# Attention scores of two transformer blocks: from plain fp32 matmuls head by head to three fp32r passes over high and low parts

## The chip, the cores and the metric

One core of a Trainium2 chip runs the whole kernel. The metric is device microseconds of one execution. Engines are called as in the profile: PE is TensorE's matmuls, PEld its weight loads, DVE is VectorE, ACT is ScalarE, POOL is GpSimd, SP issues most DMAs.

## What is computed

One sequence of 256 tokens, width 1024, passes through two blocks, all in fp32. The first block mixes with two attentions of 8 heads of 64 and gates them, then runs a layer that picks experts by product keys (PEER). The second block mixes with a causal attention and a gated spatial unit, then runs a gated feed-forward of 2816. The scores are three einsums:

```python
# first block, sliding window: 8 query heads on 2 key heads
logits = jnp.einsum('bcqhgd,bckhd->bhgcqk', qc, kw) * (HEAD_DIM ** -0.5)
logits = logits - slopes[None, :, :, None, None, None] * dist
probs = jax.nn.softmax(jnp.concatenate([logits, sink], axis=-1), axis=-1)[..., :-1]
# first block, stick-breaking: 8 heads
z = jnp.einsum('bqhd,bkhd->bhqk', q_blk, k) * (dh ** -0.5)
log_beta = jax.nn.log_sigmoid(z)
log_keep = jnp.where(before, jax.nn.log_sigmoid(-z), 0.0)
suffix = lax.cumsum(log_keep, axis=3, reverse=True) - log_keep
weights = jnp.where(before, jnp.exp(log_beta + suffix), 0.0)
# second block: with 256 tokens and blocks of 256, plain causal attention of 8 heads
s = jnp.einsum('bhqd,bhqnkd->bhqnk', qc, kg) * scale
p = jax.nn.softmax(jnp.where(mask, s, NEG_INF_2), axis=-1)
```

## The kernel before

The tokens are two blocks of 128 (NB = 2). Weights stream in units of 512 KB: `load` (line 80) issues the DMA on SP, ACT copies the unit into a high part in fp32r (line 91) and DVE takes the rest as a low part (line 92). Every projection is three fp32r matmuls, high by high, high by low, low by high (`mm3`, lines 97 to 100), feature-major (`fm`, 256 columns a matmul) or token-major (`tm`, 512 columns). `split` (line 123) makes the same two parts of an activation.

The scores alone are plain fp32. Queries and keys stand transposed, features on partitions, and two heads share the 128 partitions: head group g = 0 has partitions 0 to 63, g = 1 has 64 to 127. `swa(b, g)` (line 284), `sticks(b, g)` (line 318) and `attend(b, g)` (line 792) each take a query block b and four heads. For each head they issue one fp32 matmul of 64 rows and then a 16-bit matmul of 128 rows that adds the mask (for the sliding window the slope times distance, lines 293, 327 and 800). Block b reads n = 128 (b + 1) keys. The scores of four heads fill one double bank of the accumulator memory, tag "lg", of which there are two; the banks "mm" (two) serve the projections and "ms" (two) the transposes.

After the scores come the softmax (DVE maximum, ACT exponentials) or, in `sticks`, two sigmoids on ACT and a scan and a product on DVE. A `tail` then transposes the weights (`weighted`, line 266), multiplies them with the values into the same double bank, and splits the result into yaH, yaL or ybH, ybL.

The order in the first block: `qkb(i)` makes queries (i < 2) and keys (i >= 2, times the token's scale `rrow`) of the stick-breaking heads; `head_norm` and `head_turn` those of the sliding window. Two swa calls stand between the qkb units; then the values (pv), then a loop of eight steps, each with a tail, the scores of a later group, and a `gate_pair(i)`: two feature-major units whose products leave the bank by a DVE multiplication (line 363) and a sigmoid. In the second block the projections 0 (queries), 1 (keys), 4 (z), 3 (u) and 2 (values) run in this order; `rope` turns queries and keys; the scores of block 0 stand behind projection 4, those of block 1 behind projection 3.

The order on each engine is fixed at build time: a scheduler takes, of the instructions that it holds ready, the one that comes first in the program, so matmuls of a gate pair fill the gaps that attention leaves. `tc.issue_after` and `tc.high_priority` bend that order.

Of the kernel before, what the change touches and what calls it, by code (L numbers as in the profile page):

```python
# [9 lines left out]
F32 = mybir.dt.float32  # L10
# [8 lines left out]
P = 128  # L19
# [27 lines left out]
def block_kernel(ctx, tc, a, out):  # L47
# [101 lines left out]
    # ================= mixer of the first block =================  # L149
    with tc.tile_pool(name="b1", bufs=1) as b1:  # L150
# [30 lines left out]
        def x_part(i):  # L181
            # two chunks of the features of all tokens, times their gains
# [41 lines left out]
        qkn = b1.tile([P, NB, 10, HD], F32, name="qkn")  # L224
        va = b1.tile([P, NB, 2 * HD], F32, name="va")
        qaT = b1.tile([P, 4, S], F32, tag="qaT", name="qaT")
        kaT = b1.tile([P, S], F32, name="kaT")
        qkbT = b1.tile([P, 8, S], F32, tag="qkbT", name="qkbT")
        vb = b1.tile([P, NB, 512], F32, tag="vb", name="vb")
# [3 lines left out]
        ybH = b1.tile([P, 4, S], F32R, name="ybH")  # L233
        ybL = b1.tile([P, 4, S], F32R, name="ybL")
# [19 lines left out]
        def head_turn(b):  # L254
# [29 lines left out]
        def swa(b, g):  # L284
            # heads 4g .. 4g + 3 read key head g
            n = P * (b + 1)
            t = slice(b * P, b * P + P)
            r = slice(64 * g, 64 * g + 64)
            tile_ = pair()
            lg = quarters(tile_)  # L290
            for i in range(4):
                pe.matmul(lg[:, i, 0:n], qaT[r, i, t], kaT[r, 0:n], start=True, stop=False)  # L292
                pe.matmul(lg[:, i, 0:n], slopes[:, 4 * g + i, :], dist[:, b, 0:n], start=False,
                          stop=True)
            sm = b1.tile([P, 6, 4], F32, tag="sm", bufs=3, name="sm")
            sk = sinks[:, 4 * g:4 * g + 4]
            dve.tensor_reduce(sm[:, 0, :], lg[:, :, 0:n], axis=AX.X, op=ALU.max)
            dve.tensor_tensor(sm[:, 0, :], sm[:, 0, :], sk, op=ALU.max)
            dve.tensor_scalar_mul(sm[:, 1, :], sm[:, 0, :], -1.0)
            dve.tensor_sub(sm[:, 2, :], sk, sm[:, 0, :])  # L300
            pr = t4([P, 4, S], name="pr")
            act.activation(sm[:, 3, :], sm[:, 2, :], AF.Exp)
            for i in range(4):
                act.activation(pr[:, i, 0:n], lg[:, i, 0:n], AF.Exp, bias=sm[:, 1, i:i + 1],
                               accum_out=sm[:, 4, i:i + 1])
            dve.tensor_tensor(sm[:, 4, :], sm[:, 4, :], sm[:, 3, :], op=ALU.add)
            dve.reciprocal(sm[:, 5, :], sm[:, 4, :])

            def tail():
                y = tile_[:, 0, 0:256]  # L310
                weighted(pr, b + 1, lambda sb, i: va[:, sb, g * HD:g * HD + HD], y)
                ys = b1.tile([P, 4, HD], F32, tag="ys", bufs=2, name="ys")
                dve.tensor_tensor(ys, y.rearrange("p (h d) -> p h d", d=HD),
                                  sm[:, 5, :, None].to_broadcast([P, 4, HD]), op=ALU.mult)
# [3 lines left out]
        def sticks(b, g):  # L318
            # heads g, g + 2, g + 4, g + 6
            n = P * (b + 1)  # L320
            t = slice(b * P, b * P + P)
            r = slice(64 * g, 64 * g + 64)
            tile_ = pair()
            lg = quarters(tile_)
            for i in range(4):
                pe.matmul(lg[:, i, 0:n], qkbT[r, i, t], qkbT[r, 4 + i, 0:n], start=True, stop=False)  # L326
                pe.matmul(lg[:, i, n - P:n], identb, strict, start=False, stop=True)
            keep, beta, suf = t4([P, 4, S]), t4([P, 4, S]), t4([P, 4, S])
            pool.memset(suf[:, :, n - 1:n], 1.0)
            act.activation(keep[:, :, 0:n], lg[:, :, 0:n], AF.Sigmoid,  # L330
                           scale=rms8[:, b, 1:2])
            act.activation(beta[:, :, 0:n], lg[:, :, 0:n], AF.Sigmoid,
                           scale=rms8[:, b, 0:1])
            for i in range(4):
                dve.tensor_tensor_scan(suf[:, i, 0:n - 1][:, ::-1], keep[:, i, 1:n][:, ::-1],
                                       zero[:, 0:n - 1], 1.0, op0=ALU.mult, op1=ALU.add)
# [810 lines left out]
```

## Time and profile before

| | |
|---|---|
| timed runs | 1322.13, 1322.47, 1324.13 us; median 1322.47 us |
| profiled execution, span from the first to the last instruction | 1319.7 us |
| its own time | not listed beside the span; the median of the timed runs lies 2.8 us above the span |
| PE / PEld / DVE / ACT / POOL busy | 1295.5 / 1168.7 / 847.7 / 712.4 / 36.7 us |
| mean granted clock of TensorE | 0.994 of full speed |

Busy time adds up an engine's instructions, overlaps left out. A matmul's row shows its whole passage through the array; matmuls overlap one another, so the price of one in a stream is the distance from its start to the next start. "PEclk" is the granted clock, 1.00 for 2.4 GHz. What ended an engine's idle time is written behind the row as [idle <- releaser].

### The profile page before, as it was taken

How to read it: one execution, taken by the hardware profiler on the slowest of the kernel's cores; microseconds unless marked ns; L12 is line 12 of the kernel's file. 1: busy time of each engine (PE TensorE's matmuls, PEld its weight loads, DVE VectorE, ACT ScalarE, POOL GpSimd, SP SyncE). 2: the span in 40 equal slices, each digit the busy share in tenths (PEclk: the TensorE clock that was granted, in tenths of full speed). 3: DMA queues.
4: the chain of work that ended last, by engine and by line, in shares of the span. 5: the costliest groups of instructions: out<-in, count | busy, mean ns of one | idle time of the engine just before them, and what ended most of it. 6: DMA issues, size and time to landing. Idle time of an engine off the chain costs nothing.

```text
span 1319.7 us, 21851 instructions
## 1 busy us (share of the span) xinstructions
PE 1295.5 (98%) x8612; PEld 1168.7 (89%) x8612; DVE 847.7 (64%) x1440; ACT 712.4 (54%) x1166; POOL 36.7 (3%) x44
## 2 busy tenths in 40 slices
PE   8999999999999999999999999999999999999997
PEld 7888978999999999999988888888887778899996
DVE  5555685499987777777655555555555757545555
ACT  6474454444558777777544444544453464444443
POOL 2200000000000000000000000000000121000000
PEclk9999999999999999999999999999999999999999
DMA  8532464544555444454565665565666544455552
GB/s 297 176 96 96 138 214 149 190 153 159 184 161 179 157 161 160 160 161 160 178 195 196 195 194 192 191 193 194 193 197 202 192 147 151 150 179 189 189 181 94
DMA packets 65478, 229.11 MB, mean 174 GB/s; under 512 B 8288, under 2 KB 9056, under 8 KB 65248
## 3 DMA queue, kind: packets, MB, share of 16 engines
q1 hardware_dynamic: 64800, 226.54, 52.5%
q8 instruction: 67, 1.10, 0.3%
q10 hardware_dynamic: 576, 1.18, 0.3%
q14 instruction: 35, 0.29, 0.1%
HBM read 226.64 MB, written 1.05 MB: 173 GB/s over the span
## 4 chain that ended last, share of the span: by engine, by line
PE 89%; DVE 6%; ACT 2%; DMA 2%; issue 1%; POOL 0%; POOLq 0%; DVEq 0%; ACTq 0%
PE ps_mm L98 15%; PE ps_mm L100 15%; PE ps_mm L99 15%; PE ps_lg L99 12%; PE ps_lg L98 12%; PE ps_lg L100 12%; DVE wl L92 2%; PE ps_lg L655 1%; PE ps_lg L657 1%; PE ps_ms L132 1%; PE ps_lg L281 1%; DMA raw<-in_w_dram 1%; PE ps_lg L799 1%; PE ps_lg L292 1%; PE ps_lg L326 1%
## 5 line engine op out<-in xcount | busy, mean ns | idle before, releaser
L92 DVE TENSOR_TENSOR wl<-raw,wh 128x1024 fp32r<-128x1024 f32 (+1 forms) x385 | 470.9, 1226 | 328.5 <-ACT wh L91 327.7
L91 ACT ACTIVATE wh<-raw 128x1024 fp32r<-128x1024 f32 (+1 forms) x385 | 405.0, 1053 | 431.1 <-PE ps_lg L99 212.2
L98 PE MATMUL ps_mm<-xh,wh 128*128 128x256 f32 x1408 | 401.8, 285 | 0.0
L100 PE MATMUL ps_mm<-xh,wl 128*128 128x256 f32 x1408 | 398.6, 283 | 2.0 <-DVE wl L92 1.9
L99 PE MATMUL ps_mm<-xl,wh 128*128 128x256 f32 x1408 | 398.3, 283 | 0.0
L100 PEld LDWEIGHTS ps_mm<-xh,wl 128*128 128x128 f32 x1408 | 269.8, 192 | 2.6 <-DVE wl L92 2.6
L99 PEld LDWEIGHTS ps_mm<-xl,wh 128*128 128x128 f32 x1408 | 270.0, 192 | 0.7
L98 PEld LDWEIGHTS ps_mm<-xh,wh 128*128 128x128 f32 x1408 | 269.8, 192 | 0.7
L98 PE MATMUL ps_lg<-wh,sp 128*128 128x512 f32 x496 | 193.0, 389 | 0.0
L99 PE MATMUL ps_lg<-wl,sp 128*128 128x512 f32 x496 | 193.0, 389 | 0.0
L100 PE MATMUL ps_lg<-wh,sp 128*128 128x512 f32 x496 | 192.9, 389 | 0.0
L100 PEld LDWEIGHTS ps_lg<-wh,sp 128*128 128x128 f32 x496 | 93.1, 188 | 19.4
L99 PEld LDWEIGHTS ps_lg<-wl,sp 128*128 128x128 f32 x496 | 93.1, 188 | 19.3
L98 PEld LDWEIGHTS ps_lg<-wh,sp 128*128 128x128 f32 x496 | 93.1, 188 | 19.1
L641 ACT ACTIVATE oh<-oh,gL 128x128 f16<-128x128 f16 x256 | 83.6, 429 | 2.2 <-DVE oh L639 1.9
L98 PE MATMUL ps_mm<-hh,wh 128*128 128x256 f32 x192 | 56.1, 292 | 1.8 <-DVE gates L363 1.8
L100 PE MATMUL ps_mm<-hh,wl 128*128 128x256 f32 x192 | 55.0, 286 | 0.5 <-DVE wl L92 0.5
L99 PE MATMUL ps_mm<-hl,wh 128*128 128x256 f32 x192 | 54.7, 285 | 0.0
L125 DVE TENSOR_TENSOR sp<-store,sp 128x512 fp32r<-128x512 f32 x62 | 42.4, 684 | 0.2 <-ACT sp L124 0.2
L98 PEld LDWEIGHTS ps_mm<-hh,wh 128*128 128x128 f32 x192 | 36.6, 191 | 3.0 <-DVE gates L363 2.4
L124 ACT ACTIVATE sp<-store 128x512 fp32r<-128x512 f32 x62 | 38.0, 613 | 0.4 <-DVE store L668 0.4
L626 ACT ACTIVATE store<-ps_mm 128x512 f32<-128x512 f32 (+31 forms) x60 | 27.1, 451 | 19.6 <-DVE store L624 15.0
(369 smaller groups left out, 1701.8 us busy)
## 6 DMA issues: line engine op xcount, KB each, us to landing
raw<-in_u_dram SPq DMA_DIRECT2D x128, 512.0 KB, 3.5
raw<-in_v_dram SPq DMA_DIRECT2D x128, 512.0 KB, 3.3
raw<-in_wgu_dram SPq DMA_DIRECT2D x44, 512.0 KB, 3.4
raw<-in_wa_dram SPq DMA_DIRECT2D x32, 512.0 KB, 3.7
raw<-in_wd_dram SPq DMA_DIRECT2D x22, 512.0 KB, 3.4
raw<-in_w_dram SPq DMA_DIRECT2D x20, 512.0 KB, 4.5
raw<-in_wo_dram SPq DMA_DIRECT2D x16, 512.0 KB, 3.4
raw<-in_wq_dram SPq DMA_DIRECT2D x16, 512.0 KB, 4.5
```

Of the source, the lines that this page charges most:

```text
L91: act.activation(wh[:, c], raw[:, c], AF.Copy)
L92: dve.tensor_sub(wl[:, c], raw[:, c], wh[:, c].bitcast(F32))
L98: pe.matmul(dst, lh, rh, start=start, stop=False)
L99: pe.matmul(dst, lh, rl, start=False, stop=False)
L100: last_mm[0] = pe.matmul(dst, ll, rh, start=False, stop=stop)
L124: act.activation(dh, src, AF.Copy)
L125: dve.tensor_sub(dl, src, dh.bitcast(F32))
L132: pe.transpose(pt[:, i, :], src[:, (g + i) * P:(g + i) * P + P], ident)
L281: pe.matmul(y[:, i * HD:i * HD + HD], pts[sb][:, i, :], vs(sb, i), start=sb == 0, stop=sb == nsb - 1)
L292: pe.matmul(lg[:, i, 0:n], qaT[r, i, t], kaT[r, 0:n], start=True, stop=False)
L626: act.activation(store_view(2 * jp, 2, slice(done, S)), pq[:, :, done:S], AF.Gelu)
L641: act.activation(el[:, t // 2, :, t % 2], ea[:, t // 2, :, t % 2], AF.Copy, scale=gL[:, GT * c + t:GT * c + t + 1])
```

## The change

Queries and keys are kept as a high part (fp32r) and a low part. Each score is the sum of three matmuls of 64 rows: high by high, high by low, low by high. The functions take a query block with all eight heads: first the masks of both head groups, then head by head the three passes, each for g = 0 and then g = 1. In `sticks` and `attend` one mask matmul covers two heads. Both double banks are held by one block. The tails of a block run one after the other. `attend` splits into scores with weights, and a later `turn` that transposes. The order around them is written out again. Comments are dropped; tiles change places (qkn shares a tag with vb, ybH and ybL take those of qaH and qaL, the kept query weights those of qkbH and qkbL).

```diff
+    def logits(lgs, masks, q, k, n):
+        for g in range(2):
+            masks(g, lgs[g])
+        for i in range(4):
+            for j, (a_, b_) in enumerate(((0, 0), (0, 1), (1, 0))):
+                for g in range(2):
+                    pe.matmul(lgs[g][:, i, 0:n], q(g, i)[a_], k(g, i)[b_], start=False,
+                              stop=j == 2, skip_group_check=True)
...
         def head_turn(b):
...
-            act.activation(qaT[:, :, t], pt, AF.Copy, scale=0.125)
             pt2 = bank("ms")
             pe.transpose(pt2[:, 0:P], qf[:, 512:640], ident)
-            dve.tensor_copy(kaT[:, t], pt2[:, 0:P])
+            act.activation(qaH[:, :, t], pt, AF.Copy, scale=0.125)
+            act.activation(kaH[:, t], pt2[:, 0:P], AF.Copy)
+            dve.scalar_tensor_tensor(qaL[:, :, t], pt, 0.125, qaH[:, :, t].bitcast(F32),
+                                     op0=ALU.mult, op1=ALU.subtract)
+            dve.tensor_sub(kaL[:, t], pt2[:, 0:P], kaH[:, t].bitcast(F32))
...
-        def sticks(b, g):
+        def sticks(b):
...
-            for i in range(4):
-                pe.matmul(lg[:, i, 0:n], qkbT[r, i, t], qkbT[r, 4 + i, 0:n], start=True, stop=False)
-                pe.matmul(lg[:, i, n - P:n], identb, strict, start=False, stop=True)
+            def masks(g, lg):
+                for i in range(0, 4, 2):
+                    pe.matmul(lg[:, i:i + 2, n - P:n], identb,
+                              strict[:, None, :].to_broadcast([P, 2, P]), start=True, stop=False,
+                              skip_group_check=True)
+            logits(lgs, masks, lambda g, i: (qkbH[r[g], i, t], qkbL[r[g], i, t]),
+                   lambda g, i: (qkbH[r[g], 4 + i, 0:n], qkbL[r[g], 4 + i, 0:n]), n)
...
         def qkb(i):
...
-            if i < 2:
-                act.activation(qkbT[:, 2 * i:2 * i + 2, :], pq, AF.Copy)
-            else:
-                dve.tensor_tensor(qkbT[:, 2 * i:2 * i + 2, :], pq,
-                                  rrow[:, None, :].to_broadcast([P, 2, S]), op=ALU.mult)
+            f = slice(2 * i, 2 * i + 2)
+            if i >= 2:
+                pk = b1.tile([P, 2, S], F32, tag="sq", bufs=2, name="pk")
+                dve.tensor_tensor(pk, pq, rrow[:, None, :].to_broadcast([P, 2, S]), op=ALU.mult)
+                pq = pk
+            split(qkbH[:, f, :], qkbL[:, f, :], pq)
...
-        t_a = swa(0, 0)
         qkb(3)
         with tc.issue_after(last_mm[0].ins):
             head_turn(1)
-        t_b = swa(0, 1)
+        turn = swa(0)
+        vb = b1.tile([P, NB, 512], F32, tag="vb", name="vb")
         pv = [bank("mm") for _ in range(NB)]
...
-        for i in range(8):
-            tails.pop(0)()
-            if i < 6:
-                tails.append(steps[i]())
-            gate_pair(i)
+        both(turn)
+        gate_pair(0)
+        turn = swa(1)
+        gate_pair(1)
...
+        both(turn)
+        gate_pair(2)
+        turn = sticks(0)
+        gate_pair(3)
+        both(turn)
+        gate_pair(4)
+        turn = sticks(1)
+        gate_pair(5)
+        gate_pair(6)
+        both(turn)
+        gate_pair(7)
...
     def rope(src, b, part, scale):
...
-        act.activation(dst[:, :, b * P:b * P + P], pt, AF.Copy, scale=scale)
+        h, l = (x[:, part, :, b * P:b * P + P] for x in (qkH, qkL))
+        act.activation(h, pt, AF.Copy, scale=scale)
+        dve.scalar_tensor_tensor(l, pt, scale, h.bitcast(F32), op0=ALU.mult, op1=ALU.subtract)
...
-    for b in range(NB):
-        z_chain(b)
-    at = [attend(0, 0), attend(0, 1)]
+    zst = [z_stats(b) for b in range(NB)]
     up = [bank("mm") for _ in range(NB)]
-    proj(3, up)
+    proj(3, up, range(0, 2))
+    at = attend(0)
+    proj(3, up, range(2, 4))
+    with tc.issue_after(zst[1][1].ins):
+        for b in range(NB):
+            z_scale(b, zst[b][0])
+    at = [turn() for turn in at]
     for b in range(NB):
         act.activation(us[:, b], up[b], AF.Gelu)
-    at += [attend(1, 0), attend(1, 1)]
+    vp = [bank("mm") for _ in range(NB)]
+    proj(2, vp, range(0, 1))
+    turns = attend(1)
+    proj(2, vp, range(1, 3))
     z_mix(0)
     z_mix(1)
+    proj(2, vp, range(3, 4))
...
-    vp = [bank("mm") for _ in range(NB)]
-    proj(2, vp)
+    at += [turn() for turn in turns]
```

`swa` and `attend` change as `sticks` does; in `swa` the masks stay one matmul a head, with n columns.

## Rows read from the trace of the kernel before

**Rows 1.** The page: busy time of each engine, and the chain that ended last, by engine.

```profile
PE 1295.5 (98%) x8612; PEld 1168.7 (89%) x8612; DVE 847.7 (64%) x1440; ACT 712.4 (54%) x1166; POOL 36.7 (3%) x44
...
PE 89%; DVE 6%; ACT 2%; DMA 2%; issue 1%; POOL 0%; POOLq 0%; DVEq 0%; ACTq 0%
```

**Rows 2.** The waits of PE: what it waited for, total us, times, longest.

```profile
PE ps_mm L98 <- DVE gates L363: 1.8, 3, 0.9
```

**Rows 3.** Busy time by stretch: length, then for each engine busy us and number of instructions, granted clock, DMA share, GB/s.

```profile
20.00:44.00 24.00, 23.51 (x197) 23.31 (x197) 14.91 (x20) 14.40 (x23) 12.82 (x12) 1.00 0.72 227
...
66.00:97.00 31.00, 30.99 (x220) 25.79 (x218) 15.30 (x33) 22.02 (x42) 0.11 (x1) 1.00 0.28 86
97.00:132.00 35.00, 33.79 (x243) 28.63 (x241) 19.70 (x34) 17.31 (x26) 0.00 (x0) 1.00 0.32 105
...
1045.00:1075.00 30.00, 30.00 (x125) 21.10 (x124) 19.65 (x28) 17.36 (x34) 11.54 (x6) 0.90 0.44 145
```

**Rows 4.** The score lines, one by one: instructions, ns (least, median, most), first and last start, shapes.

```profile
L292 PE MATMUL ps_lg<-kaT,qaT x32: 272/374/480, 44.9 to 82.8; 64*128 64x128 f32 x16, 64*128 64x256 f32 x16
...
L326 PE MATMUL ps_lg<-qkbT x32: 272/374/480, 92.4 to 128.5; 64*128 64x128 f32 x16, 64*128 64x256 f32 x16
...
L799 PE MATMUL ps_lg<-qkT x32: 272/376/579, 1047.9 to 1071.8; 64*128 64x128 f32 x16, 64*128 64x256 f32 x16
```

**Rows 5.** Timeline of PE, stick-breaking, block 0, first head group: start, length, engine, line, operation.

```profile
92.38 0.48 PE L326 MATMUL ps_lg<-qkbT 64*128 64x128 f32 x2
92.80 0.23 PE L327 MATMUL ps_lg<-strict,identb 128*128 128x128 bf16 x1
92.96 0.48 PE L326 MATMUL ps_lg<-qkbT 64*128 64x128 f32 x2
...
94.57 0.36 PE L99 MATMUL ps_mm<-hl,wh 128*128 128x256 f32 x1
```

**Rows 6.** The same view for 256 columns: the sliding window, block 1, then stick-breaking, block 1.

```profile
70.01 0.70 PE L292 MATMUL ps_lg<-kaT,qaT 64*128 64x256 f32 x2
...
70.85 0.70 PE L292 MATMUL ps_lg<-kaT,qaT 64*128 64x256 f32 x2
...
113.71 0.70 PE L326 MATMUL ps_lg<-qkbT 64*128 64x256 f32 x2
...
114.50 0.70 PE L326 MATMUL ps_lg<-qkbT 64*128 64x256 f32 x2
```

**Rows 7.** Timeline of PE and PEld in plain streams: fp32r with 256 columns, fp32r with 512, fp32 weight loads of transposes, 16-bit matmuls with 128.

```profile
95.25 0.28 PE L98 MATMUL ps_mm<-hh,wh 128*128 128x256 f32 x1
...
95.37 0.28 PE L99 MATMUL ps_mm<-hl,wh 128*128 128x256 f32 x1
...
61.67 0.39 PE L98 MATMUL ps_mm<-wh,hh 128*128 128x512 f32 x1
61.89 0.39 PE L99 MATMUL ps_mm<-wl,hh 128*128 128x512 f32 x1
...
95.86 0.90 PEld L272 LDWEIGHTS ps_ms<-ident,pr 128*128 128x128 f32 x8
...
621.56 0.22 PE L655 MATMUL ps_lg<-oh 128*128 128x128 f16 x1
621.62 0.22 PE L657 MATMUL ps_lg<-oh 128*128 128x128 f16 x1
```

**Rows 8.** Busy time by stretch around the second block's scores, columns as in rows 3 (the granted clock is the third number from the end). The rows of 1053 and 1054 have the clock 0.50 too.

```profile
1051.00:1052.00 1.00, 1.00 (x7) 0.57 (x6) 1.00 (x5) 0.00 (x0) 0.11 (x1) 0.86 0.03 12
1052.00:1053.00 1.00, 1.00 (x5) 0.78 (x5) 0.40 (x1) 0.50 (x1) 1.00 (x1) 0.50 0.00 0
...
1055.00:1056.00 1.00, 1.00 (x5) 0.80 (x4) 1.00 (x3) 0.94 (x6) 1.00 (x1) 0.93 0.00 0
...
1072.00:1074.00 2.00, 2.00 (x7) 1.49 (x7) 1.23 (x1) 0.30 (x1) 0.00 (x0) 0.55 1.02 379
1074.00:1076.00 2.00, 2.00 (x7) 1.60 (x6) 1.21 (x2) 1.98 (x2) 0.00 (x0) 0.60 0.27 111
```

**Rows 9.** Timeline of PE: the first scores of the second block, two matmuls of the projection behind them, and the first and last of its block 1.

```profile
1047.89 0.49 PE L799 MATMUL ps_lg<-qkT 64*128 64x128 f32 x2
...
1053.76 0.63 PE L100 MATMUL ps_mm<-wh,xl 128*128 128x512 f32 x1
1054.18 0.63 PE L98 MATMUL ps_mm<-wh,xh 128*128 128x512 f32 x1
...
1065.98 0.70 PE L799 MATMUL ps_lg<-qkT 64*128 64x256 f32 x2
...
1072.13 0.25 PE L800 MATMUL ps_lg<-causal,identb 128*128 128x128 bf16 x1
```

**Rows 10.** Timeline of ACT and DVE: one sigmoid, the scans, a gate product and the weights' product of stick-breaking, block 1, one head group; and the keys' product of qkb.

```profile
116.97 1.12 ACT L330 ACTIVATE t<-ps_lg,rms 128x1024 f32<-128x1024 f32 x1 [2.77 <-PE ps_lg L327]
...
118.12 2.43 DVE L335 TENSOR_TENSOR_SCAN t<-t,zero 128x255 f32<-128x255 f32 x4 [3.36 <-ACT t L330]
...
120.46 0.40 DVE L363 TENSOR_TENSOR gates<-ps_mm,rrow 128x256 f32<-128x256 f32 x1
120.78 1.22 DVE L337 TENSOR_TENSOR t<-t,t 128x1024 f32<-128x1024 f32 x1
...
43.40 0.69 DVE L355 TENSOR_TENSOR qkbT<-ps_mm,rrow 128x512 f32<-128x512 f32 x1 [0.69 <-PE ps_mm L100]
```

More of the change, by code (lines that the diff above doesn't have):

```diff
@@ L223, in block_kernel @@
             dve.tensor_copy(rrow[:, b * P:b * P + P], pr_[:, 0:P])
-        qkn = b1.tile([P, NB, 10, HD], F32, name="qkn")
+        qkn = b1.tile([P, NB, 10, HD], F32, tag="vb", name="qkn")
         va = b1.tile([P, NB, 2 * HD], F32, name="va")
[L226 to L229, printed above, removed]
+        qaH = b1.tile([P, 4, S], F32R, tag="qaH", name="qaH")
+        qaL = b1.tile([P, 4, S], F32R, tag="qaL", name="qaL")
+        kaH = b1.tile([P, S], F32R, name="kaH")
+        kaL = b1.tile([P, S], F32R, name="kaL")
+        qkbH = b1.tile([P, 8, S], F32R, tag="qkbH", name="qkbH")
+        qkbL = b1.tile([P, 8, S], F32R, tag="qkbL", name="qkbL")
         gates = b1.tile([P, 16, S], F32, tag="gates", name="gates")
@@ L282, in weighted, with swa @@
                               start=sb == 0, stop=sb == nsb - 1)
-        def swa(b, g):
+        def swa(b):
             n = P * (b + 1)
             t = slice(b * P, b * P + P)
-            r = slice(64 * g, 64 * g + 64)
-            tile_ = pair()
-            lg = quarters(tile_)
-            for i in range(4):
[L292 to L311, printed above, removed]
@@ new lines, in swa @@
+            r = [slice(64 * g, 64 * g + 64) for g in range(2)]
+            tiles = [pair(), pair()]
+            lgs = [quarters(x) for x in tiles]
+            def masks(g, lg):
+                for i in range(4):
+                    pe.matmul(lg[:, i, 0:n], slopes[:, 4 * g + i, :], dist[:, b, 0:n],
+                              start=i % 2 == 0, stop=False, skip_group_check=True)
+            logits(lgs, masks, lambda g, i: (qaH[r[g], i, t], qaL[r[g], i, t]),
+                   lambda g, i: (kaH[r[g], 0:n], kaL[r[g], 0:n]), n)
@@ new lines, in sticks, with masks @@
+            r = [slice(64 * g, 64 * g + 64) for g in range(2)]
+            tiles = [pair(), pair()]
+            lgs = [quarters(x) for x in tiles]
+            def masks(g, lg):
+                for i in range(0, 4, 2):
[4 more added lines that the diff above has]
+                   lambda g, i: (qkbH[r[g], 4 + i, 0:n], qkbL[r[g], 4 + i, 0:n]), n)
@@ new lines, in sticks @@
+            betas = []
+            for g in range(2):
+                lg = lgs[g]
+                keep, beta, suf = t4([P, 4, S]), t4([P, 4, S]), t4([P, 4, S])
+                pool.memset(suf[:, :, n - 1:n], 1.0)
+                act.activation(keep[:, :, 0:n], lg[:, :, 0:n], AF.Sigmoid,
+                               scale=rms8[:, b, 1:2])
+                act.activation(beta[:, :, 0:n], lg[:, :, 0:n], AF.Sigmoid,
+                               scale=rms8[:, b, 0:1])
+                for i in range(4):
+                    dve.tensor_tensor_scan(suf[:, i, 0:n - 1][:, ::-1], keep[:, i, 1:n][:, ::-1],
+                                           zero[:, 0:n - 1], 1.0, op0=ALU.mult, op1=ALU.add)
+                dve.tensor_tensor(beta[:, :, 0:n], beta[:, :, 0:n], suf[:, :, 0:n], op=ALU.mult)
+                betas.append(beta)
@@ L396, in block_kernel, with both @@
             act.activation(vb[:, b], pv[b], AF.Copy, scale=rms[:, b, 3:4])
[L397 to L404 removed]
+        def both(tail):
+            tail(0)
+            tail(1)
+        both(turn)
+        gate_pair(0)
+        turn = swa(1)
+        gate_pair(1)
+        ybH = b1.tile([P, 4, S], F32R, tag="qaH", name="ybH")
+        ybL = b1.tile([P, 4, S], F32R, tag="qaL", name="ybL")
+        both(turn)
[9 more added lines that the diff above has]
+        gate_pair(7)
         mh = b1.tile([P, KD, S], F32R, tag="hh", name="mh")
@@ L442, in block_kernel @@
         w01 = b1.tile([P, 4, 1024], F32R, tag="gates", name="w01")
-        w2_ = b1.tile([P, 2, 1024], F32R, tag="qkbT", name="w2_")
-        w3 = [b1.tile([P, 1024], F32R, tag=t, name="w3") for t in ("vb", "qaT")]
-        places = [(w01[:, 0], w01[:, 1]), (w01[:, 2], w01[:, 3]), (w2_[:, 0], w2_[:, 1]), w3]
+        w2_ = b1.tile([P, 2, 1024], F32R, tag="qkbH", name="w2_")
+        w3 = b1.tile([P, 2, 1024], F32R, tag="qkbL", name="w3")
+        places = [(w01[:, 0], w01[:, 1]), (w01[:, 2], w01[:, 3]), (w2_[:, 0], w2_[:, 1]),
+                  (w3[:, 0], w3[:, 1])]
         units = [load(a["wq"][i], places[i]) for i in range(4)]
@@ L769, in block_kernel, with proj, rope @@
     ym = t4([P, NB, 512], name="ym")
-    qkT = b2.tile([P, 2, 4, S], F32, tag="mh", name="qkT")
-    def proj(n, dst):
-        for i in range(4):
+    qkH = b2.tile([P, 2, 4, S], F32R, tag="mh", name="qkH")
+    qkL = b2.tile([P, 2, 4, S], F32R, tag="ml", name="qkL")
+    def proj(n, dst, units=range(4)):
+        for i in units:
             tm(load(w2[4 * n + i]), 2 * i, dst, xh, xl)
-    def rope(src, b, dst, scale):
+    def rope(src, b, part, scale):
         v = src.rearrange("p (h d) -> p h d", d=HD)
```

102 lines of the change are left out of this document (58 added, 44 removed).

## The prediction, made before the changed kernel was run

> **What bounds the kernel now.** The first view is the page's busy time and chain: TensorE's matmuls cover 1295.5 of a span of 1319.7 us, and the chain that ended last is 89% PE [rows 1]. The kernel is a stream of matmuls with few holes, so what the change takes out of or puts into that stream moves the end, as long as no other engine comes late. The second view, the waits, says how late others are: the wait that the edited stage owns is 1.8 us in three pieces, matmuls of the gates held by VectorE's reading of the gate bank [rows 2]. The third view, busy time by stretch, says what cover the other engines have: VectorE is busy 14.9 of 24 us and 15.3 of 31 us and 19.7 of 35 us around the first block's attention, and 19.7 of 30 us in the second block's [rows 3]. The score matmuls lie in three places, lines 292, 326 and 799, and each line has 32 instructions for 16 matmuls in the code, half with 128 and half with 256 columns [rows 4]: every plain fp32 matmul runs as two instructions.
>
> **Cost of the scores before.** The timeline of a block of four heads shows head after head: a pair of 64-row instructions, then a mask of 128 rows, then the next head. With 128 columns a head takes 0.58 us (92.38 to 92.96) [rows 5], with 256 columns 0.79 us (113.71 to 114.50), and in the sliding-window heads, whose mask has 256 columns too, 0.84 us (70.01 to 70.85) [rows 6]. The step from 128 to 256 columns is 0.21 us, 1.66 ns a column, or four cycles at 2.4 GHz. What is left of a head after its columns (0.58 less 0.21) is 0.36 us, of which 0.05 is the mask's own columns; so going into the 64-row shape and back out costs about 0.31 us a head. There are 24 heads of each width: 24 x 0.575 + 8 x 0.84 + 16 x 0.787 = 33.1 us. Around a block of four lies about 0.1 us more (94.57 less 92.38 is 2.19 us, and the weights of the matmul that follows are late too [rows 5]); ten such stretches make 1.0 us. Before: 34.1 us.
>
> The shape change is where a page speaks: the Trainium skill, TensorEngine Tiling (Array Packing), Key Properties, says that changing the tiling mode drains TensorE, and that changing only the tile does not. The first half agrees with the 0.31 us a head; the second half is about the alternation that no row shows.
>
> **Cost of the scores after.** Masks: 8 of 128 columns or 8 of 256 in the sliding window, 4 of 256 in each of the other four blocks. A 16-bit matmul of 128 columns with its own weights starts 0.058 us after the one before, a 256-column stream 0.12 us [rows 7]: 8 x 0.058 + 8 x 0.12 + 16 x 0.12 = 3.3 us. Shape changes: one pair for each of six blocks in place of one a head, 6 x 0.31 = 1.9 us, and 6 x 0.1 around them. The three passes: 6 blocks x 24 = 144 matmuls of 64 rows in fp32r, half with 128 and half with 256 columns.
>
> No row shows such a matmul, so I bound it. Nearest rows: fp32r of 128 rows starts every 0.12 us with 256 columns and every 0.227 us with 512, one cycle a column [rows 7]. Fp32 weight loads, 128 columns each, follow one another at 0.10 us ((0.90 - 0.19) / 7) [rows 7]. From above, with the halves in single file at 256 columns 0.12 us, and at 128 columns the fp32 price of four cycles, 0.213 us; from below, both halves at once, half of 0.12 and of 0.107. I take 0.107 us for both widths: the weight loads are what the trace never shows closer than 0.10, and every one of the 144 has its own. That is 15.4 us. After: 3.3 + 1.9 + 0.6 + 15.4 = 21.2 us, 12.9 us less than before.
>
> **The clock.** In the second block the granted clock falls while the heads run: 0.86, then 0.50 for three rows, then 0.93 (1051 to 1056), and again 0.55 and 0.60 (1072 to 1076) [rows 8]. 0.50 is the 1.2 GHz level. The loss is the missing part of each row: 0.14 + 3 x 0.50 + 0.07 = 1.7 us, and 2 x 0.45 + 2 x 0.40 = 1.7 us. A 512-column matmul then takes 0.43 us from start to start (1053.76 to the next) instead of 0.227 [rows 7, 9]. The falls came after eight heads in a row, 3.8 us and 6.1 us of this pattern (1047.89 to 1051.7, 1065.98 to 1072.1) [rows 9]; four heads in a row, 3.4 us at most, left the clock at 1.00 [rows 3]. After the change the 64-row part of a block is 24 x 0.107 = 2.6 us, with far fewer holes. I expect both falls gone: 3.4 us less.
>
> **The splits, and what hides them.** Queries and keys now need a low part: VectorE gets a 128x512 operation of 0.69 us (the size of row 355) [rows 10] four times in qkb, twice in head_turn (its small copy of keys becomes a small difference) and four times in rope, 6.9 us in all; ScalarE gets four copies, about 2 us (two of 512 columns, at half of the 1.12 us of line 330's 1024 [rows 10], and two of 128). The cover is VectorE's idle time, 9 us of the 24 and 10 of the 30 us stretch [rows 3]; without it they would be 7 us on the path. None is read by the next matmul in the order: pv's 48 matmuls of 512 columns (10.9 us) stand behind the last head_turn, 48 of proj(4) behind the last rope. Taken at 0, bound 0 to +2.
>
> **The order.** A block now takes both double banks of scores and holds them until both tails are done, so the next block's scores wait for two tails; gate matmuls stand in between and can be taken first. What is queued behind: in VectorE's queue both head groups' scans and products (2.43 + 1.22 us each with 256 columns) may come in one piece ahead of line 363, the gate product that PE waited for at 120.46 [rows 10]. Against it, two gate pairs, 96 matmuls or 11.5 us, stand between the scores and the tails of the last block. ybH in qaH's place, vb in qkn's, and the wq units in qkbH and qkbL free after their readers, well before they are written. The later half of the diff (the second block's proj, z_stats, z_scale) moves instructions that all stay, and SP's loads keep their order (units of projections 4, 3, 2); PE is already busy for the whole 30.0 us there [rows 3], so apart from the clock there is no hole to fill. Taken at 0; from -1.8 (the waits of rows 2 gone) to +5.
>
> **Sum.** 12.9 + 3.4 = 16.3 us less. The profiled span of 1319.7 us becomes 1303.4; the median of the timed runs, 1322.5, lies 2.8 us over the span, and with this unchanged the forecast is **1306.2 us**.
>
> **Rivals.**
> *Halves at once.* The alternation lets the upper 64 rows run while the lower run, loads and streams both: 72 x 0.06 + 72 x 0.054 = 8.2 us in place of 15.4, so 1299 us. For it: the halves read other partitions and write other banks (lgs[0], lgs[1]). Against: the trace has no two loads closer than 0.10 us in fp32. The Trainium skill, TensorE: Matmul & The Clock Gate, Part 3: Packing small matmuls — row/col tiling, states that matmuls in different row groups run concurrently; by that this would be the case, and no run here shows it yet.
>
> *128 columns get no fp32r rate.* Then 72 of the matmuls cost 0.213 us: +7.6 us, 1314 us; a 128-column block would be 5.1 us of 64-row work, longer than the 3.8 after which the clock fell, so up to three falls of 1.7 us, 1319 us. For: no 128-column fp32r is in the trace. Against: at 256 and 512 columns it is one cycle a column.
>
> *The tails come late.* Both groups' scans in one piece of 7.3 us against two gate banks of work (5.8 us), twice in stick-breaking, and both groups' exponentials in one piece: +5 us, 1311 us. For: line 363 already held PE three times. Against: gate matmuls between.
>
> *Slower: each turn of halves drains.* If going from rows 0-63 to 64-127 costs what a shape change costs, x for each of 144 matmuls: at x = 0.11 the gain of 16.3 is gone, and at 0.15 (half of the 0.31 pair) it is +21.6 us, and blocks of 6.2 us bring the clock down again, at least the 3.4: 1331 us. For: the 64-row pair now waits for its weights after each change. Against: that change is between 64 and 128 rows, this one is not; the page of the skill named above says that a change of tile alone does not drain.
>
> **The numbers.** Forecast (1302 to 1310) 0.42, halves at once 0.32, late tails 0.13, no fp32r rate at 128 columns 0.08, draining turns 0.05. A measurement of this kernel can tell about 0.2%, 2.6 us, from no change. Faster: the first three whole and half of the fourth, 0.91; same: 0.02 of the fourth and 0.01 of the last, 0.03; slower: the rest, 0.06. The range reaches from below the halves at once to the tails and the lower end of the fourth: 1296 to 1316; outside are the last case, most of the fourth, and the edges, under 2 in 10.
>
> **What would show it.** Right: the score lines become three-pass rows of 64 rows with starts near 0.107 us at either width, masks ahead of them in one piece, and clock 1.00 between 1040 and 1080. Starts near 0.06 mean halves at once; 0.21 at 128 columns the third; 0.2 and more at both widths the last. Waits of PE on line 363's product or on the tails that grow beyond 1.8 us show the order. The prediction is wrong if matmuls outside the scores got longer, or if the holes of PE grow by more than the scores shrink.

## The result and the profile after

The changed kernel takes 1310.5 us (median of 4 runs, 1308.0 to 1311.8) against 1322.5 us; the ratio is 0.9915, 95% interval 0.9898 to 0.9933. Faster by 12.0 us, where 16.3 were forecast. The time lies in the range, but terms of the sum were wrong by more than the 4.3 us between, with opposite signs: the scores became cheaper than forecast, new waits took that back and more, and the gain that was forecast from the clock did not come.

The first view of after is the page's busy time and chain, to be read beside [rows 1].

```profile
span 1310.0 us, 21930 instructions
PE 1279.8 (98%) x8644; PEld 1164.7 (89%) x8644; DVE 854.2 (65%) x1450; ACT 710.2 (54%) x1168; POOL 37.0 (3%) x44
...
PE 86%; DVE 7%; ACT 3%; DMA 2%; issue 1%; POOL 1%; POOLq 0%; DVEq 0%; ACTq 0%
```

PE's busy time fell by 15.7 us (1295.5 to 1279.8), its idle time rose by 6.0 (span less busy: 24.2 to 30.2): -9.7 us of span. The medians differ by more, 12.0 us: wherever a run's time and span are both on record, the time lies 1.7 to 1.8 us above the span, so the profiled execution of before (1319.7) was about 1 us quicker than its median, and that of the changed kernel was the slowest of its four (1311.8). The chain of work passes through DVE and ACT for 2% more.

The scores themselves, PE's timeline in stick-breaking, block 0 (128 columns), and block 1 (256 columns), beside [rows 5, 6]; the last lines are the projection's matmuls around block 1:

```profile
95.66 0.27 PE L149 MATMUL ps_lg<-qkbL,qkbH 64*128 64x128 f32 x1
95.67 0.27 PE L149 MATMUL ps_lg<-qkbH 64*128 64x128 f32 x1
95.77 0.27 PE L149 MATMUL ps_lg<-qkbH,qkbL 64*128 64x128 f32 x1
95.78 0.27 PE L149 MATMUL ps_lg<-qkbL,qkbH 64*128 64x128 f32 x1
...
114.29 0.28 PE L100 MATMUL ps_mm<-hh,wl 128*128 128x256 f32 x1
...
115.32 0.28 PE L149 MATMUL ps_lg<-qkbH 64*128 64x256 f32 x1
115.32 0.28 PE L149 MATMUL ps_lg<-qkbL,qkbH 64*128 64x256 f32 x1
115.43 0.28 PE L149 MATMUL ps_lg<-qkbH,qkbL 64*128 64x256 f32 x1
...
116.12 0.38 PE L98 MATMUL ps_mm<-hh,wh 128*128 128x256 f32 x1
116.34 0.28 PE L99 MATMUL ps_mm<-hl,wh 128*128 128x256 f32 x1
```

Two matmuls, one of each half, start within 0.01 us of each other, and the next two 0.11 us (128 columns) or 0.12 us (256 columns) later: 0.056 and 0.06 us a matmul. So the halves run at once, the first rival. The 144 passes cost 36 x 0.111 + 36 x 0.119 = 8.3 us instead of 15.4.

Going into the 64-row shape and out of it comes on top. In block 1 the projection's next matmul was due at 114.41 (114.29 and 0.12) and starts at 116.12, and the one behind it starts 0.22 us later instead of 0.12: 1.81 us, of which 12 x 0.119 = 1.43 are the passes' starts and 0.38 the way in and out. Counted in this way over every stretch of masks and scores, with waits and the low clock taken out, they cost 15.5 us in the changed kernel and 33.3 in the kernel before (34.1 in the prediction's sum): 17.8 us less, where 12.9 were forecast.

The waits of PE, beside [rows 2] (what was waited for, total us, times, longest), first two more of before, then those of the changed kernel:

```profile
PE ps_ms L132 <- DVE x L742: 2.5, 1, 2.5
...
PE ps_lg L98 <- DVE x L437: 1.9, 1, 1.9
```

```profile
PE ps_ms L876 <- ACT pr L865: 4.5, 1, 4.5
PE ps_mm L98 <- DVE gates L395: 2.9, 2, 1.9
PE ps_lg L98 <- DVE x L482: 2.6, 1, 2.6
...
PE ps_lg L295 <- ACT ptt L289: 0.9, 1, 0.9
```

L876 transposes the softmax weights of the second block's block 0, L395 is the gate product that was L363, L295 multiplies the sliding window's weights with the values. The first and the last wait are new, the gates' grew from 1.8, and the third, L437 before, from 1.9. The 2.5 us of L742 became 1.4 (L788).

The granted clock by stretch (the third number from the end), beside [rows 8]:

```profile
80.00:100.00 20.00, 19.12 (x156) 18.17 (x154) 11.37 (x23) 13.26 (x28) 0.11 (x1) 0.91 0.32 106
120.00:140.00 20.00, 18.12 (x140) 17.66 (x140) 13.77 (x20) 9.01 (x14) 0.00 (x0) 0.91 0.33 107
180.00:200.00 20.00, 16.89 (x74) 13.16 (x73) 12.10 (x19) 7.12 (x15) 1.11 (x2) 0.91 0.31 103
1040.00:1060.00 20.00, 15.46 (x82) 11.22 (x81) 13.75 (x20) 9.77 (x23) 9.92 (x6) 0.91 0.37 125
1060.00:1080.00 20.00, 20.00 (x121) 16.93 (x120) 13.05 (x18) 15.90 (x34) 0.94 (x1) 0.92 0.52 176
```

Before, three stretches of 20 us stood at 0.91, one at 1000 to 1020 and two around the second block's scores; the rest was 1.00 but for the last, in which the kernel ends. Now five do, three of them in the first block. Taking (1 - clock) x 20 over all stretches, 12.0 us are lost where 8.2 were. In the changed kernel each fall comes behind one of the waits above: at 87 behind the 0.9 us, at 124 behind the 1.9 of the gates, at 186 behind the 2.6, at 1056 behind the 4.5. Of the three falls before, the one at 1007 came behind the wait of 2.5 us that ends at 1006.0; the two at the scores had no wait ahead of them.

These sums are of one execution each. Over the timed runs that list it, the mean granted clock is 0.988 to 0.997 for the kernel before (25 runs, median 0.992) and 0.992 to 0.994 for the changed one (8 runs, median 0.993). So it is not shown that the change makes the clock slower; it is shown that the gain of 3.4 us did not come.

The wait of 4.5 us, in DVE's timeline:

```profile
1050.33 1.77 DVE L922 TENSOR_TENSOR zs<-zs,zst 128x512 f32<-128x512 f32 x1 [1.76 <-POOL zst L139]
1052.02 1.27 DVE L859 TENSOR_REDUCE sm<-ps_lg 128x4 f32<-128x512 f32 x2
1053.22 1.24 DVE L860 TENSOR_SCALAR sm<-sm 128x4 f32<-128x4 f32 x1
```

The scores end at 1046.2, but the maximum (L859) starts at 1052.0. Ahead of it in DVE's queue stands a product of z_scale (L922), which waits for a power on POOL. Only then come the negation, the exponentials and PE's transposes, at 1056.35.

The gate product (L395) in stick-breaking's block 1, in the same view:

```profile
117.27 2.43 DVE L365 TENSOR_TENSOR_SCAN t<-t,zero 128x255 f32<-128x255 f32 x4 [0.42 <-ACT t L360]
...
120.98 2.42 DVE L365 TENSOR_TENSOR_SCAN t<-t,zero 128x255 f32<-128x255 f32 x4
123.32 0.40 DVE L395 TENSOR_TENSOR gates<-ps_mm,rrow 128x256 f32<-128x256 f32 x1
```

It stands behind the scans of both head groups; PE goes on at 123.77, after the wait of 1.9 us.

### The profile page after: what moved, and what is told of

Read it like the earlier page. It is cut to its first block, busy times and chain, and to the rows that moved or that the text cites. A ratio compares the mean times of both kernels' runs of the same rounds, so it can differ in the third digit from the quotient of the medians.

```text
span 1310.0 us, 21930 instructions
## 1 busy us (share of the span) xinstructions
PE 1279.8 (98%) x8644; PEld 1164.7 (89%) x8644; DVE 854.2 (65%) x1450; ACT 710.2 (54%) x1168; POOL 37.0 (3%) x44
## 4 chain that ended last, share of the span: by engine, by line
PE 86%; DVE 7%; ACT 3%; DMA 2%; issue 1%; POOL 1%; POOLq 0%; DVEq 0%; ACTq 0%
PE ps_mm L98 15%; PE ps_mm L100 15%; PE ps_mm L99 15%; PE ps_lg L98 12%; PE ps_lg L99 12%; PE ps_lg L100 12%; DVE wl L92 2%; PE ps_lg L701 1%; PE ps_lg L703 1%; PE ps_lg L295 1%; PE ps_ms L132 1%; ACT wh L91 1%; PE ps_lg L149 1%; DVE t L365 1%; PE ps_ms L557 0%
## 5 line engine op out<-in xcount | busy, mean ns | idle before, releaser
L91 ACT ACTIVATE wh<-raw 128x1024 fp32r<-128x1024 f32 (+1 forms) x385 | 404.8, 1054 | 429.5 <-PE ps_lg L99 210.5
L100 PEld LDWEIGHTS ps_mm<-hh,wl 128*128 128x128 f32 x192 | 37.8, 197 | 0.3 <-DVE wl L92 0.2
```

Source lines behind the costliest of these rows:

```text
L91: act.activation(wh[:, c], raw[:, c], AF.Copy)
L100: last_mm[0] = pe.matmul(dst, ll, rh, start=False, stop=stop)
```

## The experiments

"Idle" is span less PE's busy time in the profiled execution, "clock" the loss as summed above (about 3 us of it is the kernel's end in each). A ratio is to the kernel before, timed beside the run: its median was 1321.0 us on the chip of e5 to e8 and 1322.7 or 1322.8 on that of the other experiments, so times of the two groups are compared by their ratios.

| kernel | median us | ratio, 95% interval | idle us | clock us |
|---|---|---|---|---|
| before | 1322.5 | | 24.2 | 8.2 |
| changed | 1310.5 | 0.9915, 0.9898 to 0.9933 | 30.2 | 12.0 |
| e1_masks_first | 1312.6 | 0.9922, 0.9903 to 0.9941 | 29.3 | 6.8 |
| e6_passes_alone | 1311.5 | 0.9924, 0.9897 to 0.9950 | 25.7 | 11.6 |
| e2_half_after_half | 1312.9 | 0.9929, 0.9909 to 0.9949 | 28.9 | 8.2 |
| e5_fp32_in_turns | 1306.2 | 0.9889, 0.9863 to 0.9915 | 26.5 | 8.6 |
| e3_z_behind_max | 1305.4 | 0.9875, 0.9856 to 0.9893 | 27.3 | 8.6 |
| e4_gate_first | 1308.2 | 0.9890, 0.9874 to 0.9906 | 29.2 | 10.2 |
| e7_three_orders | 1300.9 | 0.9850, 0.9824 to 0.9875 | 25.2 | 3.0 |
| e8_three_orders_fp32 | 1301.9 | 0.9852, 0.9827 to 0.9878 | 26.7 | 4.6 |
| e9_orders_half_after_half | 1309.2 | 0.9900, 0.9882 to 0.9918 | 25.7 | 4.8 |
| e10_changed_again | 1311.3 | 0.9908, 0.9892 to 0.9925 | 30.0 | 12.0 |

### What each part is worth: e1_masks_first, e6_passes_alone

e1 is the kernel before with only the masks of a block of four heads moved ahead of its plain fp32 scores (the same in `sticks` and `attend`):

```diff
-                pe.matmul(lg[:, i, 0:n], qaT[r, i, t], kaT[r, 0:n], start=True, stop=False)
-                pe.matmul(lg[:, i, 0:n], slopes[:, 4 * g + i, :], dist[:, b, 0:n], start=False,
-                          stop=True)
+                pe.matmul(lg[:, i, 0:n], slopes[:, 4 * g + i, :], dist[:, b, 0:n],
+                          start=i % 2 == 0, stop=False, skip_group_check=True)
+            for i in range(4):
+                pe.matmul(lg[:, i, 0:n], qaT[r, i, t], kaT[r, 0:n], start=False, stop=True,
+                          skip_group_check=True)
```

> The kernel before with one edit: in each block of four heads the four masks are issued first and then the four plain fp32 score matmuls; nothing else of the change. Theory (going into the 64-row shape and back out costs 0.31 us a head): 48 such changes become 12, 36 x 0.31 = 11.2 us less, about 1311 us, with the pairs of a head 0.21 us (128 columns) and 0.43 us (256 columns) apart. Rival (the gain of the change is in the three passes and the turns of halves, the masks' places are hidden): 1320 to 1323 us. If the low clock in the second block's scores came from the shape changes it is gone here, up to 3.4 us more.

Measured 1312.6 us: 10.1 us less than the 1322.7 of before on that chip. Its scores, PE's timeline in the sliding window's block 0 and block 1:

```profile
44.85 1.16 PE L295 MATMUL ps_lg<-kaT,qaT 64*128 64x128 f32 x8
...
68.26 1.99 PE L295 MATMUL ps_lg<-kaT,qaT 64*128 64x256 f32 x8
```

Eight plain fp32 instructions, four heads, take 1.16 us with 128 columns and 1.99 us with 256 (starts 0.127 and 0.223 us apart), where a head took 0.58 and 0.84 us each with its mask [rows 5, 6]. Counted as above, masks and scores take 23.3 us, 10.0 less than before. So the shape change that the prediction priced at 0.31 us a head is real, and taking it out alone brings most of what the whole change brought. That the time fell by just as much has two more terms in it, which nearly cancel: PE's idle time rose by 5.1 us, and the granted clock of the four runs is 0.996 to 0.997 against a median of 0.992 before, by estimate 6 us (0.0045 x 1320).

The idle time is a wait like the changed kernel's, in the old order and without the passes, at the second block's block 1; PE's waits, then ACT's timeline:

```profile
PE ps_ms L824 <- ACT pr L816: 4.2, 1, 4.2
```

```profile
1064.27 1.06 ACT L91 ACTIVATE kept<-raw 128x1024 fp32r<-128x1024 f32 x1 [6.98 <-DMA raw<-in_wo_dram]
```

The exponentials stand in ACT's queue behind the split of a unit of the output projection (`kept`) whose DMA lands late. So such a wait comes with shorter scores in the old order too; the new order is not its only cause.

e6 adds the three passes and the splits to e1, in the old order, one head group at a time:

```diff
+                for j, (q_, k_) in enumerate(((qaH, kaH), (qaH, kaL), (qaL, kaH))):
+                    pe.matmul(lg[:, i, 0:n], q_[r, i, t], k_[r, 0:n], start=False, stop=j == 2,
+                              skip_group_check=True)
```

> The kernel before, in its own order, with masks first for each block of four heads (as in the masks-first run) and with the three passes and the splits; one head group at a time, so the halves never run at once. Single file, pitches 0.111 and 0.120 us from the run with one half after the other: 24 x 0.333 + 24 x 0.360 = 16.6 us, against 16.8 us of the plain fp32 scores of the masks-first run. Theory 1, the passes themselves are worth nothing and the splits cost nothing: 1312.6 us, within 2 us. Theory 2, the splits come on the path: up to 7 us more, 1319 us. Theory 3, three passes are a third cheaper than fp32 (three cycles a column for four): 1308 us.

Measured 1311.5 us, its ratio 0.9924 beside e1's 0.9922: within the intervals, some 4 us, the passes are worth nothing by themselves, and the splits cost nothing there. In single file three passes cost 0.333 us a head where fp32 costs 2 x 0.127 = 0.254 with 128 columns; with 256 it is 0.36 against 0.446. The two widths nearly cancel (16.6 and 16.8 us for the 24 heads of each).

### The turns of the halves: e2_half_after_half, e5_fp32_in_turns

e2 is the changed kernel with the loop over the head groups outermost:

```diff
-        for i in range(4):
-            for j, (a_, b_) in enumerate(((0, 0), (0, 1), (1, 0))):
-                for g in range(2):
+        for g in range(2):
+            for i in range(4):
+                for j, (a_, b_) in enumerate(((0, 0), (0, 1), (1, 0))):
```

> The changed kernel with one edit: all twelve score matmuls of head group 0 first, then the twelve of group 1, so the halves don't turn. Theory (halves at once): starts 0.107 to 0.12 us apart in place of 0.056, 144 x 0.055 = 8 us more, about 1318 us. Rival (each half alone would run as fast, the weight loads of one half are hidden as well): 1310.5 us, starts 0.055 at 128 columns. It also shows the price of a 64-row fp32r matmul of 128 columns by itself: 0.107 if the weights bind, 0.21 if the narrow ones get no fp32r rate.

```profile
49.63 0.27 PE L149 MATMUL ps_lg<-kaL,qaH 64*128 64x128 f32 x1
49.74 0.27 PE L149 MATMUL ps_lg<-kaH,qaL 64*128 64x128 f32 x1
...
73.70 0.28 PE L149 MATMUL ps_lg<-kaL,qaH 64*128 64x256 f32 x1
73.82 0.28 PE L149 MATMUL ps_lg<-kaH,qaL 64*128 64x256 f32 x1
```

PE's timeline of e2 shows single file at 0.111 and 0.120 us: the 0.107 of the prediction was right for one half, and with the turns it does twice as much. Where group 1 follows group 0, though, the halves overlap here too:

```profile
50.41 0.27 PE L149 MATMUL ps_lg<-kaH,qaL 64*128 64x128 f32 x1
50.42 0.38 PE L149 MATMUL ps_lg<-kaH,qaH 64*128 64x128 f32 x2
50.58 0.33 PE L149 MATMUL ps_lg<-kaL,qaH 64*128 64x128 f32 x2
...
50.81 0.27 PE L149 MATMUL ps_lg<-kaH,qaH 64*128 64x128 f32 x1
```

From 50.42 to 50.81 the passes of both groups run in pairs. So a block costs 0.7 to 1.1 us more than in turns, near 6 us in all, not 8. The time rose by only 2.4 us (1312.9), within the intervals. This is about the kernel that the sum of the prediction describes, and it should then have come out at 1306.

e5 keeps order and turns and puts one plain fp32 matmul in place of three passes, without low parts and splits:

```diff
-            for j, (a_, b_) in enumerate(((0, 0), (0, 1), (1, 0))):
-                for g in range(2):
-                    pe.matmul(lgs[g][:, i, 0:n], q(g, i)[a_], k(g, i)[b_], start=False,
-                              stop=j == 2, skip_group_check=True)
+            for g in range(2):
+                pe.matmul(lgs[g][:, i, 0:n], q(g, i), k(g, i), start=False, stop=True,
+                          skip_group_check=True)
```

> The changed kernel with its order and its turns of the halves, but with one plain fp32 matmul a head in place of the three passes, and no low parts and no splits. From the masks-first run a plain fp32 instruction of 64 rows costs 0.127 us with 128 columns and 0.223 us with 256, two a matmul. Theory 1, the halves run at once whatever the type: 24 x 0.127 + 24 x 0.223 = 8.4 us for the 48 scores, against 24 x 0.167 + 24 x 0.177 = 8.3 us for the 144 passes: 1310.5 us, the same within 2 us; the rows come in pairs with starts 0.127 and 0.223 us apart. Theory 2, only the fp32r passes run at once: the fp32 instructions stand in single file, 16.8 us; the run that put the halves one after the other lost 2.4 us on 8 us more of scores, so 1313 us or, if nothing of it is absorbed, 1319 us.

```profile
49.77 1.16 PE L148 MATMUL ps_lg<-kaH,qaH 64*128 64x128 f32 x16
...
72.44 2.00 PE L148 MATMUL ps_lg<-kaH,qaH 64*128 64x256 f32 x16
```

Sixteen instructions in the time of e1's eight: fp32 runs in both halves at once as well. The time is 1306.2 us, not the 1310.5 expected: by the ratios 3.4 us better than the changed kernel, with intervals that overlap, and with scores of the same price. What the trace shows of it is the order, which the scheduler lays out anew without the splits: both maxima of block 0 come ahead of the second product of z_scale, and PE's wait for the exponentials is 1.5 us instead of 4.5.

### What came back: e3_z_behind_max, e4_gate_first

e3 queues z_scale's products on DVE behind the last negation of block 0's softmax:

```diff
-        dve.tensor_scalar_mul(sm[:, 1, :], sm[:, 0, :], -1.0)
+        last_max[0] = dve.tensor_scalar_mul(sm[:, 1, :], sm[:, 0, :], -1.0)
...
-    with tc.issue_after(zst[1][1].ins):
+    with tc.issue_after(zst[1][1].ins), tc.issue_after(last_max[0].ins):
```

> The changed kernel with one edit: VectorE's two z_scale products are ordered behind the second maximum's negation of attend(0), so the maxima no longer stand in the queue behind a product that waits for GpSimd's power. Theory: the maximum runs right behind the scores, some 6 us earlier, the wait of PE of 4.5 us falls below 1, and at least one of the two low-clock stretches behind it (1.7 us each) goes: 1303 to 1306 us. Rival (exponentials and table load on ScalarE set the tails anyway): the wait shrinks by 1 or 2 us only, 1308 to 1310 us. If the scores themselves bring the clock down, it falls at the same place without the wait.

```profile
PE ps_ms L878 <- ACT pr L867: 2.0, 1, 2.0
```

Measured 1305.4 us, 5.1 less than the changed kernel; the wait (L876 there) fell from 4.5 to 2.0, not below 1 as expected, and 1060 to 1080 is at 1.00 again. What is left of it stands in ACT's timeline of e3:

```profile
1050.61 1.06 ACT L91 ACTIVATE kept<-raw 128x1024 fp32r<-128x1024 f32 x1 [5.16 <-DMA raw<-in_wo_dram]
```

The maxima are there at 1048.2, but ACT's next instruction splits a unit of the output projection whose DMA lands late, and the exponentials stand behind it, as in e1.

e4 takes the gate product ahead of the scans and products on DVE:

```diff
-                dve.tensor_tensor(gates[:, f, :], pg[:, j, :], rrow, op=ALU.mult)
+                with tc.high_priority(offset=200):
+                    dve.tensor_tensor(gates[:, f, :], pg[:, j, :], rrow, op=ALU.mult)
```

> The changed kernel with one edit: the gate product of gate_pair has a higher priority (200), which puts it between the two groups' scans in VectorE's queue instead of behind both. Theory (late tails: the scans in one piece hold the gate bank): the 1.9 us wait in stick-breaking's block 1 falls below 0.6 and the low clock that follows it goes too (1.7 us), about 1307.5 us. Rival (the wait goes to the tails instead, which now end later): 1309 to 1312 us.

```profile
PE ps_mm L98 <- DVE gates L396: 2.5, 3, 1.1
...
120.00:140.00 20.00, 18.54 (x155) 18.02 (x155) 14.75 (x22) 9.36 (x14) 0.00 (x0) 1.00 0.33 107
```

Measured 1308.2 us, 2.3 less, with intervals that overlap. The wait of 1.9 us became one of 0.9 and one of 0.6 (the 1.1 stands at 102, in block 0, as in the changed kernel), so it did not fall below the 0.6 expected, and the clock's fall behind it is gone. The scans did stand ahead of the product: this is the rival of the late tails.

### All three orders: e7_three_orders, e8_three_orders_fp32, e9_orders_half_after_half

e7 has e3's and e4's edits and puts the loads of the output projection with their splits, that kept unit's first among them, behind the exponentials (`last_exp` is the last one of block 0):

```diff
+            with tc.issue_after(last_exp[0].ins):
+                units[k0, half] = load(a["wo2"][4 * half + k0 // 2],
+                                       kept() if len(units) < 7 else None)
```

> The changed kernel with three orders bent: z_scale's products on VectorE behind the maxima of attend(0), the gate product ahead, and the split of the first kept unit of the output projection on ScalarE behind the last exponential of attend(0) (in the trace it waited 5.2 us there for its DMA, and the exponentials stood behind it). The first two alone gave -5.2 and -2.4 us; the third takes away the 2.0 us for which PE still waited on the exponentials and the clock's fall behind it, 1.7 us. All three add up: 1310.5 - 5.2 - 2.4 - 3.7 = 1299 us. If the orders of the first two overlap, or PE then waits for the next weights or the gelu instead: 1303 us. If the wait has nothing to do with that queue: 1303 us with the wait still at 2.0 us.

```profile
80.00:100.00 20.00, 19.13 (x169) 18.17 (x168) 11.89 (x25) 14.71 (x33) 0.11 (x1) 1.00 0.32 106
...
180.00:200.00 20.00, 17.22 (x81) 13.38 (x80) 10.86 (x18) 6.74 (x12) 1.12 (x2) 1.00 0.24 79
1040.00:1060.00 20.00, 19.37 (x123) 15.04 (x122) 12.19 (x19) 14.74 (x30) 9.05 (x6) 1.00 0.48 163
```

Measured 1300.9 us, its ratio 0.9850 beside 0.9915; its interval lies below the changed kernel's. The exponentials' wait has left the list (0.6 us on the gelu took its place), the idle time is at 25.2, near the 24.2 of before, and no stretch but the end is below 1.00. It beats both kernels.

e8 is e7 with e5's plain fp32 scores.

> The run with three orders bent, with plain fp32 scores in turns of the halves in place of the passes, no low parts and no splits (7 us less on VectorE). If the halves run at once in fp32 too, the same as that run or up to 1.5 us faster, since VectorE's queue is shorter: 1298 to 1303 us. If they do not, 8.4 us more of scores with little left that absorbs it: 1304 to 1309 us.

Measured 1301.9 us, ratio 0.9852 beside 0.9850: with the orders bent, fp32 and three passes are the same. The 1.5 us that VectorE's shorter queue might have given did not show.

e9 is e7 with e2's edit.

> The run with three orders bent, with the halves one after the other (head group 0's twelve passes, then head group 1's), as in the run that did this to the changed kernel and lost only 2.4 us of 8. Single file costs 24 x (0.333 + 0.360) = 16.6 us against 8.3 us. Theory 1, the late softmax and gate work absorbed the rest there, and with the orders bent little is left that absorbs it: 1300.9 + 8.3 less 1 to 3 us = 1306 to 1308 us. Theory 2, the passes of one head group run beside other matmuls anyway, so that single file is dearer in the rows than in time: 1303 us.

Measured 1309.2 us (1305.8 to 1312.1), 8.3 more than e7; the ratios differ by 0.0050, or 6.6 us, the spans by 6.1. The 8.3 of the expectation leaves out the overlap seen in e2: counted as above, masks and scores take 21.5 us here and 15.7 in e7, 5.8 more. So the time follows the rows here, as far as the intervals can tell (6.6 us, give or take 4). In the changed kernel 2.4 of some 6 us showed; that late softmax and gate work covered the rest there fits the waits, but no run takes it apart.

### Whether the clock's falls belong to the program: e10_changed_again

> The changed kernel once more, nothing edited. If the places where the clock falls belong to the program, its trace shows the falls of the first one again: 80 to 100, 120 to 140, 180 to 200 and a double one about 1056. If they come and go with small shifts in time, the waits are the same ones (4.5, 2.9 and 2.6 us) and some of the falls are absent or elsewhere. The time is 1310.5 us within 2 us either way.

```profile
80.00:100.00 20.00, 19.11 (x155) 18.17 (x154) 11.03 (x22) 13.58 (x29) 0.11 (x1) 0.91 0.33 106
120.00:140.00 20.00, 18.12 (x140) 17.66 (x139) 13.65 (x21) 9.13 (x14) 0.00 (x0) 0.91 0.33 107
180.00:200.00 20.00, 16.99 (x74) 13.24 (x73) 11.54 (x18) 6.57 (x14) 1.12 (x2) 0.91 0.30 97
1040.00:1060.00 20.00, 15.45 (x83) 11.29 (x83) 14.27 (x20) 9.65 (x24) 9.93 (x6) 0.92 0.40 123
1060.00:1080.00 20.00, 20.00 (x119) 16.63 (x118) 13.06 (x18) 15.89 (x33) 0.93 (x1) 0.90 0.54 176
```

Without an edit all five falls are in their places, and the time is 1311.3 us. Across kernels, though, the same wait of 0.9 us at 84 is followed by a fall in the changed kernel and in e4, and by none in e3, e5, e7 and e8. The same holds of longer waits: e9 has the gates' 2.0 us at 123, e7 2.0 us at 182 and e1 2.7 us at 186, all without a fall, and e6 has a fall at 1047 with no wait ahead of it, behind 24 passes one half at a time. So e7 lost the falls at 87 and 186 while their waits stayed. What decides was not settled: a wait goes before each fall in the changed kernel, and e4 lost a fall together with a wait, but that a wait brings the fall is not shown.

## Why the prediction was right, and where it was wrong

- **Scores before, 34.1 us, and the 0.31 us a head**: borne out, 33.3 us by the rows. e1 took out 36 x 0.31 = 11.2 us by the sum and 10.0 by its rows; the 10.1 of its time agree because idle time and clock cancelled.
- **Three passes, 15.4 us**: the mis-sized term. 0.107 us a matmul holds for one half (0.111 and 0.120 in e2), but the halves run at once: 8.3 us. The argument "no two loads closer than 0.10 us" came from loads of all 128 rows. The Trainium skill, TensorE: Matmul & The Clock Gate, Part 3: Packing small matmuls — row/col tiling, says that matmuls in different row groups run concurrently. The trace agrees: starts lie within 0.01 us. The way in and out, 2.5 us in the sum (1.9 and 0.6), was dearer: 15.5 less 8.3 less the masks' 3.3 leaves 3.9 us, for the scheduler broke three of the six blocks in two (at 94.55 two passes run, a transpose of 128 rows and two masks follow, and the shape is entered again).
- **128 columns no dearer than 256**: right, 0.111 and 0.119 us, not the 0.213 of fp32; that rival is out. Whether the weight loads set the 0.111, as the prediction argued, no run shows. **Draining turns**: out, two matmuls of the two halves start together.
- **The splits, taken at 0**: right in the old order (e6). In the new one e5 was 3.4 us faster without them, by its trace through the order of DVE's queue; with the orders bent the difference is gone (e8). They are covered, but they moved the queue.
- **The order, taken at 0 from -1.8 to +5**: the step that failed. Idle time rose by 6.0 us. The gate product waited behind both groups' scans, as the rival of the late tails said. The larger piece, 4.5 us, lay where the prediction saw "apart from the clock there is no hole to fill": z_scale and a kept unit's split came ahead of the softmax in the queues of DVE and ACT. A stretch in which PE is busy throughout says nothing of what will be ready once PE's part is shorter: e1 has such a wait in the old order.
- **The clock, -3.4 us**: did not come. The two falls behind the score pattern are gone, but others stand behind waits; in the profiled pair the loss rose from 8.2 to 12.0 us, over the timed runs the granted clock is the same within 0.001. The prediction tied the falls to the 64-row matmuls, and the three in the first block of the changed kernel have none right ahead of them: that tie was not the whole cause. The cause stays open.

Sum on the profiled spans: -17.8 (scores) + 6.0 (idle) + 3.8 (clock) = -8.0, against -9.7 measured; the 1.7 us between are not placed. From the forecast, with the clock left as it was: 1306.2 - 4.9 (scores) + 6.0 (idle) + 3.4 (clock) = 1310.7, against 1310.5; the idle time and the rows are of one execution each, so this is no closer than a few us. The halves at once and the late work were not alternatives but came together, one on each side of the forecast; that it came near is luck to that extent.

## What to carry to other kernels

Before swapping the type of a small matmul, look at what stands between them: here keeping 64-row matmuls together gave 10 us, and the change of type nothing that the runs could tell. Matmuls on rows 0 to 63 and 64 to 127, issued in turns into different banks, run at once in fp32r and in fp32. When TensorE's part shrinks, read the queues of VectorE and ScalarE for what stands ahead of the softmax: here bending three such orders gave 8 to 10 us, where an instruction early in a queue waited for POOL or a DMA, or scans stood ahead of a product that TensorE waited for.

## What was not expected of the hardware

- A negation of 128 x 4 numbers on DVE took 1.24 us (1053.22, above) where it takes 0.16 in e3 (1052.84, POOL idle), and L922's product 1.77 us where the one before it took 0.69 (1045.94, POOL idle). POOL's timeline in the changed kernel:

```profile
1050.26 1.29 POOL L923 TENSOR_TENSOR zs<-zs,lngb 128x512 f32<-128x512 f32 x1
1051.63 1.59 POOL L924 TENSOR_TENSOR zs<-zs,lngb 128x512 f32<-128x512 f32 x1
1053.18 1.26 POOL L923 TENSOR_TENSOR zs<-zs,lngb 128x512 f32<-128x512 f32 x1
```

The negation ends at 1054.46, POOL's product at 1054.44. The maxima, beside POOL's L924 at 1052 to 1053, kept their pace (two in 1.27 us). So some 1.1 us of the softmax's delay is this negation's. The Trainium skill, SBUF — State Buffer, Who interferes with whom, says that VectorE and GpSimd share a port pair as an exclusive lock, which a `tensor_scalar` or a product of two SBUF inputs can need and a `tensor_reduce` does not. The rows agree on all three.
- Plain fp32 on 64 rows runs in both halves at once too: 16 instructions in 1.16 us (e5) where one half takes 1.16 us for eight (e1).
